# A plain small unit first in every half step of a two-layer encoder, its sums spread behind it, and the first loads paired

## The chip, the cores and the metric

The kernel runs on one core of one Trainium2 chip. The metric is the device time of one execution in microseconds (us). Three runs of the kernel before took 1905.81, 1903.66 and 1898.64 us, median 1903.66 us. A profile was taken of one more execution.

## What the kernel must compute

The input x is 512 tokens of 1024 channels in float32. Each of two layers does three residual steps on it, and a last RMSNorm ends the network:

```
x = x + 0.5 * SwiGLU_1(RMSNorm(x))        # "ffn1": 1024 -> 2816 gate and up -> 1024
h = RMSNorm(x); p = h @ W_in              # pooling group, and q, k, v of 12 heads of 64
x = x + concat(pool(p), attention(p)) @ W_out
x = x + 0.5 * SwiGLU_2(RMSNorm(x))        # "ffn2": the same form, other weights
SwiGLU(h) = (silu(h @ w_gate) * (h @ w_up)) @ w_down
```

## The kernel before, in words

The residual is held transposed, as eight tiles x[0] to x[7] of 128 channels by 512 tokens. Every float32 product is made of three fp32r matmuls: each operand is split into a high part (a rounded copy, ScalarE) and a low part (the rest, VectorE). For a weight piece of 128 x 1024 these are `whi` (L374) and `wlo` (L377), made by `divide`; `take` asks for the next piece and divides two pieces ahead, and `pump` starts loads on the SyncE queue as long as buffers are free.

A SwiGLU works through its 2816 columns in six units, `UNITS` = (5, 0, 1, 2, 3, 4). Units 0 to 4 have 512 gate and 512 up columns each and use a 2 x 2 Strassen-Winograd scheme with seven products (`products`, order `PORD`); unit 5, the small unit, has 256 and 256 columns and comes first. In ffn1 it is done by `plain_unit`: four token blocks t, eight channel chunks k, three matmuls of 512 columns each, 96 in all, with four PSUM banks of tags A, A, B, B; its weights come as four pieces g of two chunks each. In ffn2 it is done by `products` with matmuls of 256 columns, 168 in all.

The Strassen products need x in parts (`Norm.fold`). For each chunk c, ScalarE first writes a scaled copy `xs` = x[c] * gain (L445). Chunks 0 to 3 give the parts `ah`, `al` of the first token half (and, in ffn1 only, `a2` of the second half). Chunks 4 to 7 give `ah`, `al` of both halves, and then at once the four sums and differences of the halves of chunks c - 4 and c: four VectorE instructions of 256 columns (L470 to L473), two ScalarE copies into `sh` (L476, L477), and two VectorE rests into `sl` (L480, L481). `ah` and `al` serve products 1, 2 and 4, and the plain unit; `sh` and `sl` serve products 6, 5, 7 and 3. `fold` runs inside the loop that finishes the step before: in `startup`, in the output projection of the mixing step (`residual`, L997), or in the last down projection (L765).

The order of instructions on each engine is the order in which the program writes them. Work that is to come a little later is put on three lists: `flush` runs the list `later`, and then `lazy` moves up to `later` and `slow` to `lazy`. `finish_col` flushes twice, then has TensorE reduce the squares (L527), VectorE add epsilon (L529) and GpSimd take the power -0.5 (L530); `activation_block` needs that result for silu (L624) and the gating product (L625), which free a PSUM bank. After the small unit its activated columns are transposed (`turn`, L632) during the unit that follows.

`startup` loads x in eight DMAs and the first four weight pieces between them, `vecs` (the gains), `col` and the positions on the GpSimd queue. It runs ten idle matmuls, then folds all eight chunks, while only the first two weight pieces are divided there; the third is divided when `plain_unit` first asks.

Of the kernel before, what the change touches and what calls it, by code (L numbers as in the profile page):

```python
# [36 lines left out]
NU = 5  # L37
# [41 lines left out]
def trunk(ctx: ExitStack, tc: tile.TileContext, a: dict):  # L79
# [20 lines left out]

    x = [const.tile([P, S], F32, name=f"x{c}") for c in range(KD)]
    vecs = const.tile([P, a["vecs"].shape[1]], F32, name="vecs")
# [16 lines left out]
    def startup(norm):  # L119
        nc.sync.dma_start(x[0], a["xT"][0])  # L120
        load(2)
        nc.gpsimd.dma_start(vecs, a["vecs"])
        nc.vector.memset(ones, 1.0 / D)
        nc.vector.memset(npow, -0.5)
        idle = const.tile([P, S], mybir.dt.bfloat16, name="idle")
        nc.vector.memset(idle, 0.0)
        nc.scalar.activation(npow, npow, AF.Copy)
        nc.sync.dma_start(x[1], a["xT"][1])
        nc.sync.dma_start(x[2], a["xT"][2])
        load(2)  # L130
# [7 lines left out]
        pos = a["positions"]  # L138
        nc.gpsimd.dma_start(col, a["col"])
        nc.gpsimd.dma_start(pos_i, bass.AP(tensor=pos.tensor, offset=pos.offset, ap=[[0, P], [1, S]]))  # L140
        warm = bank("D", "warm")
        for _ in range(WARM):
            nc.tensor.matmul(warm, idle[:, 0:P], idle, start=True, stop=True)
        for c in range(KD):
            norm.fold(c)
            if c < 4:
                divide(c % 2)
            flush()
            if c > 0:
                norm.square(c - 1)  # L150
        norm.square(KD - 1)

    def tables():
# [20 lines left out]


        nc.vector.tensor_copy(ang, pos_i)
        nc.vector.tensor_scalar(ang, ang, col[:, 0:1], None, op0=ALU.mult)
# [64 lines left out]
    def product_jobs(i, l, u):  # L242

        small = u == NU
        cps = 1 if small else 2
        made, out = {}, []

        def quarter(kh, n, cp):
            ap = a[f"gs{i}"][l, kh, n] if small else a[f"gu{i}"][l, u, kh, n, cp]
            made[kh, n, cp] = Load(ap, D)  # L250

# [62 lines left out]
    def ffn_jobs(i, l):  # L314
        for n, u in enumerate(UNITS):
            if i == 1 and u == NU:
                for g in range(4):
                    plain(("c", l, g), a["gc"][l, g], D)
# [19 lines left out]

    def load(pieces=1):
        ld = loads[state["load"]]  # L340
        ld.tile = t4([P, ld.n], F32, f"raw{state['load']}")
        state["load"] += 1
        state["live"] += 1
        state["temps"] += ld.temps
        for z in range(pieces):
            o, e = z * ld.n // pieces, (z + 1) * ld.n // pieces
            nc.sync.dma_start(ld.tile[:, o:e], ld.src[:, o:e])

# [77 lines left out]
    class Norm:  # L426
# [11 lines left out]
        def fold(self, c):  # L438

            H = S // 2  # L440
            if c == 0:
                self.xs, self.ah, self.al, self.sh, self.sl, self.a2 = ([None] * 4 for _ in range(6))
            k, nm = c % 4, f"{self.name}_{c}"
            xs = t2([P, 2, H], F32, f"xs_{nm}")
            nc.scalar.activation(xs.rearrange("p b t -> p (b t)"), x[c], AF.Copy, scale=gain(self.n, c))  # L445
            if c < 4:
                self.xs[k] = xs
                hi, lo = t3([P, 3, H], F32R, f"ah_{nm}"), t3([P, 3, H], F32R, f"al_{nm}")
                self.ah[k], self.al[k] = hi, lo
                nc.scalar.activation(hi[:, 0, :], xs[:, 0, :], AF.Copy)  # L450
                later.append(lambda: nc.vector.tensor_tensor(lo[:, 0, :], xs[:, 0, :], hi[:, 0, :].bitcast(F32),
                                                             op=ALU.subtract))
                if self.n % 3 == 0:
                    a2 = t2([P, 2, H], F32R, f"a2_{nm}")
                    self.a2[k] = a2
                    nc.scalar.activation(a2[:, 0, :], xs[:, 1, :], AF.Copy)
                    later.append(lambda: nc.vector.tensor_tensor(a2[:, 1, :], xs[:, 1, :], a2[:, 0, :].bitcast(F32),
                                                                 op=ALU.subtract))
                return
            hi, lo, x1 = self.ah[k], self.al[k], self.xs[k]  # L460
            self.xs[k] = None
            nc.scalar.activation(hi[:, 1:3, :], xs, AF.Copy)
            s13, s24 = t2([P, 2, H], F32, f"s13_{nm}"), t2([P, 2, H], F32, f"s24_{nm}")
# [4 lines left out]
            def sums():  # L468
                tt(lo[:, 1:3, :], xs, hi[:, 1:3, :].bitcast(F32), op=ALU.subtract)
                tt(s13[:, 0, :], x1[:, 1, :], xs[:, 1, :], op=ALU.subtract)  # L470
                tt(s24[:, 0, :], s13[:, 0, :], x1[:, 0, :], op=ALU.subtract)
                tt(s13[:, 1, :], x1[:, 0, :], x1[:, 1, :], op=ALU.subtract)
                tt(s24[:, 1, :], xs[:, 0, :], s24[:, 0, :], op=ALU.add)  # L473

# [141 lines left out]
    def ffn(which, l, norm, nxt, first=False):  # L616
# [20 lines left out]
        def products(n, u):  # L637
            N = S if u < NU else S // 2
            w, cps = N // 2, 2 if u < NU else 1
            xs = [bank("BA"[n % 2], f"px_{nm}_{u}_{i}") for i in range(2)]  # L640
# [7 lines left out]
            def evacuate(p):  # L648
                add, sub = ALU.add, ALU.subtract
                for i in range(2):  # L650
# [4 lines left out]
                    elif p == 2:  # L655
                        nc.vector.tensor_tensor(c[11, i], Z, c[11, i], op=add)
                        if n:
                            lazy.append(lambda i=i: activation_block(c[11, i], c[11, i], i, w))
                    elif p == 6:
                        nc.scalar.activation(new(12, i), X, AF.Copy)  # L660
                        if not n:
                            activation_block(c[11, i], c[11, i], i, w)
                    elif p == 5:
                        nc.scalar.activation(new(22, i), Z, AF.Copy)
                    elif p == 7:
                        nc.vector.tensor_tensor(c[22, i], c[22, i], X, op=sub)
                        later.append(lambda i=i: activation_block(c[22, i], c[22, i], 2 + i, w))
                    elif p == 3:
                        nc.vector.tensor_tensor(c[12, i], Z, c[12, i], op=sub)  # L669
                        later.append(lambda i=i: activation_block(c[12, i], c[12, i], i, w))  # L670
                    else:
                        activation_block(new(21, i), X, 2 + i, w)

            def step(p, cp):
# [5 lines left out]
                out = zs if p in (2, 5, 3) else xs  # L680
                ks = range(2 * cp, 2 * cp + 2) if cps == 2 else range(4)
                for i in range(2):
# [10 lines left out]
                if cp == cps - 1:  # L693
                    if not n and p == 6:
                        norm.finish_col()
                    evacuate(p)
# [4 lines left out]
            for p in PORD:  # L701
                for cp in range(cps):
                    step(p, cp)
                    if turns and z >= 1:
                        for _ in range(2):
                            if turns:
                                turns.pop(0)()
                    if n and z in DOWN_AT[last]:
                        flush()
# [9 lines left out]
            if n:  # L719
                for z, dp in enumerate(todo):  # L720
                    flush()
                    down(UNITS[n - 1], dp)
                    if last:
                        for _ in range(2):
                            flush()
                            turns.pop(0)()

        def plain_unit(u):
# [41 lines left out]
        for n, u in enumerate(UNITS):  # L770
            if n == 0 and which == 1:
                plain_unit(u)
# [384 lines left out]
```

## Time and profile before

| | us |
|---|---|
| median of three runs | 1903.66 |
| the profiled execution, as a run | 1906.05 |
| its span, first to last instruction | 1903.9 |
| TensorE busy | 1854.1 (97%) |
| VectorE busy | 1422.6 (75%) |
| ScalarE busy | 942.6 (50%) |
| mean granted TensorE clock | 0.987 |

The busy time of TensorE counts matmuls whose ends are modelled, so a share near 100% does not mean that it runs at its peak. A granted clock of 1.00 is 2.4 GHz, 0.50 is 1.2 GHz. The idle time named behind a row is that of its engine just before it, with what ended it.

### The profile page before, as it was taken

Reading aid. Unit: us, or ns where it says so; the run is one execution under the profiler, and the core shown is the slowest. Engines: PE = TensorE matmul, PEld = TensorE weight load, DVE = VectorE, ACT = ScalarE, POOL = GpSimd, SP = SyncE. Lnnn points to the kernel's source line nnn. Section 1 sums busy time; section 2 is a strip of 40 time slices with the busy share of each in tenths; the row PEclk is TensorE's granted clock in tenths of the full one; section 3 lists DMA queues with packets and bytes.
Section 4 is the critical chain, followed back from the end, with each engine's and each line's share of the span. In section 5 each row is a group of like instructions: output and inputs, shape, how many; then the busy total and the mean of one; then the engine's idle time right before and its main releaser. Section 6 shows DMA issues by size and latency. Waiting matters only on the chain.

```text
span 1903.9 us, 23219 instructions
## 1 busy us (share of the span) xinstructions
PE 1854.1 (97%) x8822; PEld 1542.4 (81%) x8822; DVE 1422.6 (75%) x2016; ACT 942.6 (50%) x1457; POOL 117.0 (6%) x105
## 2 busy tenths in 40 slices
PE   5999999999998999999999999999999989999998
PEld 4888888898877888888878888888888778888887
DVE  5898677747887886677678777766688688777675
ACT  5444444526665544344555444444467564444344
POOL 0000000014230000000000000000323100000000
PEclk8999999999999999999999999999999989999999
DMA  5322333144441232333313332330544223323321
GB/s 190 106 96 81 111 131 107 43 128 117 111 139 57 90 110 99 122 103 109 110 34 114 130 100 89 100 127 17 152 122 138 78 83 117 107 92 100 100 78 45
DMA packets 59838, 194.33 MB, mean 102 GB/s; under 512 B 7936, under 2 KB 8080, under 8 KB 59728
## 3 DMA queue, kind: packets, MB, share of 16 engines
q1 hardware_dynamic: 59584, 192.57, 31.8%
q8 instruction: 69, 1.13, 0.2%
q0 software_dynamic: 144, 0.29, 0.1%
q14 instruction: 41, 0.34, 0.1%
HBM read 171.87 MB, written 2.10 MB: 91 GB/s over the span
## 4 chain that ended last, share of the span: by engine, by line
PE 89%; DVE 7%; ACT 2%; issue 1%; DMA 0%; SPq 0%; DVEq 0%; POOLq 0%; POOL 0%; ACTq 0%
PE pd_f L401 8%; PE pd_f L400 8%; PE pd_f L399 8%; PE px_f L690 8%; PE px_f L687 8%; PE px_f L689 8%; PE pz_f L687 6%; PE pz_f L690 6%; PE pz_f L689 6%; PE pv_m L807 4%; PE ps_m L874 2%; PE pt_m L887 2%; PE pt_f L632 2%; DVE wlo L377 1%; PE pp_q_m L399 1%
## 5 line engine op out<-in xcount | busy, mean ns | idle before, releaser
L377 DVE TENSOR_TENSOR wlo<-raw,whi 128x1024 fp32r<-128x1024 f32 (+2 forms) x418 | 496.4, 1194 | 50.2 <-ACT whi L374 40.7
L374 ACT ACTIVATE whi<-raw 128x1024 fp32r<-128x1024 f32 (+2 forms) x418 | 417.9, 1024 | 222.3 <-DVE wlo L377 68.9
L401 PE MATMUL pd_f<-ah_f,wlo 128*128 128x512 f32 (+1 forms) x736 | 281.2, 382 | 2.0 <-DVE wlo L377 2.0
L399 PE MATMUL pd_f<-ah_f,whi 128*128 128x512 f32 (+1 forms) x736 | 280.8, 382 | 1.0 <-ACT ah_f L417 1.0
L400 PE MATMUL pd_f<-al_f,whi 128*128 128x512 f32 (+1 forms) x736 | 280.2, 381 | 1.0 <-DVE al_f L420 1.0
L765 DVE SCALAR_TENSOR_TENSOR x<-pd_f,x 128x512 f32<-128x512 f32 x184 | 127.0, 690 | 168.1 <-PE pd_f L401 164.6
L624 ACT ACTIVATE c_f<-c_f,rcol_n 128x256 f32<-128x256 f32 (+1 forms) x132 | 65.7, 500 | 244.4 <-DVE c_f L669 90.8
L401 PEld LDWEIGHTS pd_f<-ah_f,wlo 128*128 128x128 f32 x736 | 138.4, 188 | 32.1 <-DVE wlo L377 6.6
L400 PEld LDWEIGHTS pd_f<-al_f,whi 128*128 128x128 f32 x736 | 138.4, 188 | 28.6 <-DVE al_f L420 2.3
L399 PEld LDWEIGHTS pd_f<-ah_f,whi 128*128 128x128 f32 x736 | 138.4, 188 | 27.3 <-ACT ah_f L417 1.9
L687 PE MATMUL px_f<-whi,sh_n 128*128 128x512 f32 (+1 forms) x352 | 135.6, 385 | 1.4 <-ACT c_f L654 1.4
L690 PE MATMUL px_f<-wlo,sh_n 128*128 128x512 f32 (+1 forms) x352 | 135.3, 384 | 0.1
L689 PE MATMUL px_f<-whi,sl_n 128*128 128x512 f32 (+1 forms) x352 | 135.1, 384 | 0.0
L687 PE MATMUL pz_f<-whi,sh_n 128*128 128x512 f32 (+1 forms) x352 | 133.7, 380 | 0.0
L690 PE MATMUL px_f<-wlo,ah_n 128*128 128x512 f32 (+1 forms) x352 | 133.6, 380 | 0.0
L689 PE MATMUL px_f<-whi,al_n 128*128 128x512 f32 (+1 forms) x352 | 133.6, 379 | 0.0
L687 PE MATMUL px_f<-whi,ah_n 128*128 128x512 f32 (+1 forms) x352 | 133.6, 379 | 0.0
L690 PE MATMUL pz_f<-wlo,sh_n 128*128 128x512 f32 (+1 forms) x352 | 133.5, 379 | 0.0
L689 PE MATMUL pz_f<-whi,sl_n 128*128 128x512 f32 (+1 forms) x352 | 133.5, 379 | 0.0
L879 ACT ACTIVATE e_m<-e_m,nmx_m 128x512 f32<-128x512 f32 x96 | 69.4, 723 | 79.2 <-DVE nmx_m L877 78.6
L877 DVE CUSTOM_DVE_ANT_0 e_m<-ps_m,gbias 128x512 f32<-128x512 f32 x96 | 65.8, 686 | 33.7 <-PE ps_m L874 33.1
L530 POOL TENSOR_TENSOR rcol_n<-rcol_n,npow 128x4 f32<-128x4 f32 x6 | 6.1, 1016 | 1238.2 <-DVE rcol_n L529 1238.2
(224 smaller groups left out, 3665.8 us busy)
## 6 DMA issues: line engine op xcount, KB each, us to landing
raw<-in_gu SPq DMA_DIRECT2D x160, 512.0 KB, 3.3
raw<-in_dn SPq DMA_DIRECT2D x80, 512.0 KB, 3.3
raw<-in_wqk SPq DMA_DIRECT2D x24, 512.0 KB, 5.6
qq_m<-hl_q_m SPq DMA_DIRECT2D x48, 256.0 KB, 4.4
raw<-in_wo SPq DMA_DIRECT2D x16, 512.0 KB, 5.0
raw<-in_wv SPq DMA_DIRECT2D x16, 384.0 KB, 3.1
kk_m<-hl_k_m SPq DMA_DIRECT2D x48, 128.0 KB, 2.3
raw<-in_ds SPq DMA_DIRECT2D x16, 256.0 KB, 2.6
```

Of the source, the lines that this page charges most:

```text
L374: nc.scalar.activation(hi[:, o:e], raw[:, o:e], AF.Copy)
L377: nc.vector.tensor_tensor(lo[:, o:e], raw[:, o:e], hi[:, o:e].bitcast(F32), op=ALU.subtract)
L399: nc.tensor.matmul(ps, hi[:, o:o + P], act[0], start=start, stop=False)
L400: nc.tensor.matmul(ps, hi[:, o:o + P], act[1], start=False, stop=False)
L401: nc.tensor.matmul(ps, lo[:, o:o + P], act[0], start=False, stop=stop)
L687: nc.tensor.matmul(ps, bh, hi[:, o], start=(k == 0 and p in (1, 2, 5)), stop=False, skip_group_check=True)
L689: nc.tensor.matmul(ps, bl, hi[:, o], start=False, stop=False, skip_group_check=True)
L690: nc.tensor.matmul(ps, bh, lo[:, o], start=False, stop=(k == 3), skip_group_check=True)
L765: nc.vector.scalar_tensor_tensor(x[d], ps, 0.5, x[d], op0=ALU.mult, op1=ALU.add)
L807: nc.tensor.matmul(ps[t][:, :384], h[k][p_][:, t * P:(t + 1) * P], q_[:, o:o + 384], start=(k == 0 and n == 0), stop=(k == KD - 1 and n == 2))
L877: nc.vector.tensor_tensor_reduce(e, ps, gbias[:, o:o + S], -0.125, 3.0e38, ALU.add, ALU.min, nmx[hd][:, it:it + 1])
L879: nc.scalar.activation(e, e, AF.Exp, bias=nmx[hd][:, it:it + 1], scale=-1.0, accum_out=den[hd][:, it:it + 1])
```

## The change

In both ffn1 and ffn2 the first unit is now `plain_unit`, so the second form of the small unit is gone from `products` and from the arrays. `fold` no longer writes `xs`: the parts come straight from x with the gain as scale (ScalarE for the high part, one `scalar_tensor_tensor` on VectorE for the low part), and `a2` is made in every half step. The sums move out of `fold` into `sums(k)`, which first writes scaled copies `x1` and `x2` of chunks k and k + 4; it is called behind weight pieces 1 and 2 of the plain unit and behind token blocks 0 and 1 of its last piece. In `startup`, x[0] and x[1] are loaded in front of the two halves of the first weight piece, the other chunks in pairs of 512 KB (rows of 4 KB) with one weight piece behind each pair; the third and fourth pieces are divided in chunks 4 and 6; `col` and the positions are loaded later, in the first step of the rotary tables.

```diff
     def startup(norm):
-        nc.sync.dma_start(x[0], a["xT"][0])
-        load(2)
         nc.gpsimd.dma_start(vecs, a["vecs"])
+        load(2, first=0)
...
-        nc.sync.dma_start(x[1], a["xT"][1])
-        nc.sync.dma_start(x[2], a["xT"][2])
-        load(2)
-        nc.sync.dma_start(x[3], a["xT"][3])
-        for c in range(4, KD):
-            if c % 2 == 0:
-                load()
-            nc.sync.dma_start(x[c], a["xT"][c])
+        for c in range(1, 4):
+            nc.sync.dma_start(xp[c].rearrange("p c t -> p (c t)"), a["xT"][c])
+            load()
...
             if c < 4:
                 divide(c % 2)
+            elif c % 2 == 0:
+                divide()
...
+            def part(hi, lo, src):
+                nc.scalar.activation(hi, src, AF.Copy, scale=g)
+                later.append(lambda: nc.vector.scalar_tensor_tensor(lo, src, g, hi.bitcast(F32),
+                                                                    op0=ALU.mult, op1=ALU.subtract))
+            if c < 4:
...
+                part(self.ah[k][:, 0, :], self.al[k][:, 0, :], x[c][:, 0:H])
+                part(self.a2[k][:, 0, :], self.a2[k][:, 1, :], x[c][:, H:S])
+            else:
+                flat = lambda t: t[:, 1:3, :].rearrange("p b t -> p (b t)")
+                part(flat(self.ah[k]), flat(self.al[k]), x[c])
+
+        def sums(self, k):
+            x1, x2 = t2([P, 2, H], F32, f"x1_{nm}"), t2([P, 2, H], F32, f"x2_{nm}")
+            for t, c in ((x1, k), (x2, k + 4)):
+                nc.scalar.activation(t.rearrange("p b t -> p (b t)"), x[c], AF.Copy, scale=gain(self.n, c))
...
             for g in range(3):
                 flush()
-                w = take("c", l, g)
+                w = take("c", which, l, g)
                 for z in range(2):
                     for t in range(4):
                         part(t, 2 * g + z, w, z * S)
                     flush()
-            w = take("c", l, 3)
+                if g:
+                    norm.sums(g - 1)
+            flush()
+            w = take("c", which, l, 3)
             norm.finish_col()
...
                 activation_block(cs[t], ps[t], t, S // 2)
+                if t < 2:
+                    norm.sums(t + 2)
...
         for n, u in enumerate(UNITS):
-            if n == 0 and which == 1:
+            if n == 0:
                 plain_unit(u)
```

## Rows read from the trace of the kernel before

**Rows 1.** The page's chain that ended last, its shares by engine.
```profile
PE 89%; DVE 7%; ACT 2%; issue 1%; DMA 0%; SPq 0%; DVEq 0%; POOLq 0%; POOL 0%; ACTq 0%
```
**Rows 2.** Windows over first units: length, PE, PEld, DVE, ACT, POOL busy (instructions), clock, DMA, GB/s.
```profile
6.89:51.09 44.20, 27.64 (x105) 20.93 (x106) 28.44 (x53) 25.82 (x44) 1.03 (x1) 0.81 0.46 174
604.54:636.31 31.77, 26.19 (x178) 24.86 (x177) 26.93 (x44) 18.54 (x33) 1.02 (x1) 0.84 0.24 76
957.56:986.38 28.82, 26.13 (x105) 20.81 (x104) 19.36 (x33) 12.43 (x19) 1.01 (x1) 0.88 0.09 28
```
**Rows 3.** Windows around falls of the granted clock, and behind a plain unit.
```profile
612.90:623.10 10.20, 8.62 (x35) 7.74 (x36) 9.83 (x16) 6.20 (x11) 0.00 (x0) 0.50 0.15 51
968.60:971.70 3.10, 0.73 (x2) 0.30 (x2) 3.10 (x5) 3.10 (x4) 0.00 (x0) 0.94 0.32 85
971.70:978.10 6.40, 6.08 (x14) 4.79 (x15) 3.67 (x4) 1.20 (x2) 0.00 (x0) 0.50 0.01 3
986.38:1000.90 14.52, 14.52 (x70) 12.11 (x69) 12.92 (x13) 7.19 (x10) 0.00 (x0) 1.00 0.11 31
```
**Rows 4.** TensorE timeline (start, length, instruction), and the chain's piece for the squares.
```profile
985.70 0.39 PE L735 MATMUL pc_f<-whi,ah_n 128*128 128x512 f32 x1
986.38 0.39 PE L687 MATMUL px_f<-whi,ah_n 128*128 128x512 f32 x1
636.08 0.40 PE L687 MATMUL px_f<-whi,ah_n 128*128 128x512 f32 x1
980.15 0.79 PE ms_n L527 x8
```
**Rows 5.** VectorE timeline at the first layer's ffn2, from the first residual add on.
```profile
585.70 0.69 DVE L997 TENSOR_TENSOR x<-po_m,x 128x512 f32<-128x512 f32 x1 [4.42 <-PE po_m L401]
...
608.56 0.42 DVE L470 TENSOR_TENSOR s_n<-xs_n,xs_n 128x256 f32<-128x256 f32 x1
...
610.03 1.22 DVE L377 TENSOR_TENSOR wlo<-raw,whi 128x1024 fp32r<-128x1024 f32 x1
611.16 0.68 DVE L997 TENSOR_TENSOR x<-po_m,x 128x512 f32<-128x512 f32 x1
...
612.36 0.69 DVE L480 TENSOR_TENSOR sl_n<-s_n,sh_n 128x512 fp32r<-128x512 f32 x1
```
**Rows 6.** ScalarE: timeline of the first chunk, and two pieces of the chain.
```profile
4.85 0.72 ACT L445 ACTIVATE xs_n<-x,vecs 128x512 f32<-128x512 f32 x1 [2.61 <-DMA vecs<-in_vecs]
5.60 0.42 ACT L450 ACTIVATE ah_n<-xs_n 128x256 fp32r<-128x256 f32 x1
...
6.23 0.61 ACT L374 ACTIVATE whi<-raw 128x512 fp32r<-128x512 f32 x1
...
616.44 0.52 ACT sh_n L477
616.96 0.96 ACT whi L374
```
**Rows 7.** What follows the plain unit: power, table load, silu, first weight rest.
```profile
L530 POOL TENSOR_TENSOR rcol_n<-rcol_n,npow 128x4 f32<-128x4 f32 x6 | 6.1, 1016 | 1238.2 <-DVE rcol_n L529 1238.2
47.23 1.28 ACT L624 ACT_TABLE_LOAD   x1 [9.50 <-PE pc_f L737]
982.54 0.48 ACT L624 ACTIVATE cc_f<-pc_f,rcol_n 128x256 f32<-128x256 f32 x1 [9.49 <-PE pc_f L737]
988.04 1.22 DVE L377 TENSOR_TENSOR wlo<-raw,whi 128x1024 fp32r<-128x1024 f32 x1 [0.47 <-ACT whi L374]
```
**Rows 8.** DMA: queues (packets, MB, share) at 6 to 7 us; x[1]'s landing; a window.
```profile
q0 software_dynamic: 33, 0.12, 41.8%
q1 hardware_dynamic: 44, 0.07, 25.3%
...
x<-in_xT SPq DMA_DIRECT2D x1, 256.0 KB, 7.7
...
10.00:20.00 10.00, 8.27 (x35) 6.42 (x35) 6.41 (x14) 9.84 (x20) 0.00 (x0) 1.00 1.04 405
```

More of the change, by code (lines that the diff above doesn't have):

```diff
@@ L98, in bank @@
         return psum.tile([P, S], F32, tag=tag, name=name, bufs=2)
-    x = [const.tile([P, S], F32, name=f"x{c}") for c in range(KD)]
+    xp = [const.tile([P, 2, S], F32, name=f"x{c}") for c in range(KD // 2)]
+    x = [xp[c // 2][:, c % 2, :] for c in range(KD)]
     vecs = const.tile([P, a["vecs"].shape[1]], F32, name="vecs")
@@ L147, in startup @@
                 divide(c % 2)
+            elif c % 2 == 0:
+                divide()
             flush()
-            if c > 0:
-                norm.square(c - 1)
-        norm.square(KD - 1)
+            norm.square(c)
     def tables():
@@ L173, in reduce @@
             yield
+        pos = a["positions"]
+        nc.gpsimd.dma_start(col, a["col"])
+        nc.gpsimd.dma_start(pos_i, bass.AP(tensor=pos.tensor, offset=pos.offset, ap=[[0, P], [1, S]]))
+        yield
         nc.vector.tensor_copy(ang, pos_i)
@@ L242, in product_jobs @@
     def product_jobs(i, l, u):
-        small = u == NU
-        cps = 1 if small else 2
+        cps = 2
         made, out = {}, []
         def quarter(kh, n, cp):
-            ap = a[f"gs{i}"][l, kh, n] if small else a[f"gu{i}"][l, u, kh, n, cp]
-            made[kh, n, cp] = Load(ap, D)
+            made[kh, n, cp] = Load(a[f"gu{i}"][l, u, kh, n, cp], D)
         quarters = [(0, 0), (1, 0)]
@@ L315, in ffn_jobs @@
         for n, u in enumerate(UNITS):
-            if i == 1 and u == NU:
+            if n == 0:
                 for g in range(4):
-                    plain(("c", l, g), a["gc"][l, g], D)
+                    plain(("c", i, l, g), a[f"gc{i}"][l, g], D)
                 continue
@@ L337, in trunk, with load @@
         ffn_jobs(2, l)
-    def load(pieces=1):
+    def load(pieces=1, first=None):
         ld = loads[state["load"]]
@@ L346, in load @@
             o, e = z * ld.n // pieces, (z + 1) * ld.n // pieces
+            if first is not None:
+                nc.sync.dma_start(x[first + z], a["xT"][first, :, z * S:(z + 1) * S])
             nc.sync.dma_start(ld.tile[:, o:e], ld.src[:, o:e])
@@ L441, in fold @@
             if c == 0:
[L442 to L445, printed above, removed]
-            if c < 4:
[L447 to L459, printed above, removed]
@@ L460, in fold @@
-            hi, lo, x1 = self.ah[k], self.al[k], self.xs[k]
-            self.xs[k] = None
-            nc.scalar.activation(hi[:, 1:3, :], xs, AF.Copy)
+                self.ah, self.al, self.sh, self.sl, self.a2 = ([None] * 4 for _ in range(5))
+            k, g, nm = c % 4, gain(self.n, c), f"{self.name}_{c}"
+            def part(hi, lo, src):
+                nc.scalar.activation(hi, src, AF.Copy, scale=g)
+                later.append(lambda: nc.vector.scalar_tensor_tensor(lo, src, g, hi.bitcast(F32),
+                                                                    op0=ALU.mult, op1=ALU.subtract))
@@ L468, in sums @@
             def sums():
-                tt(lo[:, 1:3, :], xs, hi[:, 1:3, :].bitcast(F32), op=ALU.subtract)
-                tt(s13[:, 0, :], x1[:, 1, :], xs[:, 1, :], op=ALU.subtract)
+                tt(s13[:, 0, :], x1[:, 1, :], x2[:, 1, :], op=ALU.subtract)
                 tt(s24[:, 0, :], s13[:, 0, :], x1[:, 0, :], op=ALU.subtract)
                 tt(s13[:, 1, :], x1[:, 0, :], x1[:, 1, :], op=ALU.subtract)
-                tt(s24[:, 1, :], xs[:, 0, :], s24[:, 0, :], op=ALU.add)
+                tt(s24[:, 1, :], x2[:, 0, :], s24[:, 0, :], op=ALU.add)
             def parts():
@@ L656, in evacuate @@
                         nc.vector.tensor_tensor(c[11, i], Z, c[11, i], op=add)
-                        if n:
-                            lazy.append(lambda i=i: activation_block(c[11, i], c[11, i], i, w))
+                        lazy.append(lambda i=i: activation_block(c[11, i], c[11, i], i, w))
                     elif p == 6:
                         nc.scalar.activation(new(12, i), X, AF.Copy)
-                        if not n:
-                            activation_block(c[11, i], c[11, i], i, w)
                     elif p == 5:
@@ L680, in step @@
                 out = zs if p in (2, 5, 3) else xs
-                ks = range(2 * cp, 2 * cp + 2) if cps == 2 else range(4)
+                ks = range(2 * cp, 2 * cp + 2)
                 for i in range(2):
@@ L693, in step @@
                 if cp == cps - 1:
-                    if not n and p == 6:
-                        norm.finish_col()
                     evacuate(p)
@@ L707, in products @@
                                 turns.pop(0)()
-                    if n and z in DOWN_AT[last]:
+                    if z in DOWN_AT[last]:
                         flush()
@@ L718, in products @@
                         u, f, [c[top, 0], c[top, 1], c[low, 0], c[low, 1]], j, w))
[L719 to L726, printed above, removed]
+            for dp in todo:
+                flush()
+                down(UNITS[n - 1], dp)
+                if last:
+                    for _ in range(2):
+                        flush()
+                        turns.pop(0)()
         def plain_unit(u):
@@ L770, in ffn @@
         for n, u in enumerate(UNITS):
-            if n == 0 and which == 1:
+            if n == 0:
                 plain_unit(u)
@@ L1117 @@
         arrays[f"gu{i}"] = big.transpose(0, 6, 1, 7, 2, 4, 3, 5, 8).reshape(L, NU, 2, 2, 2, P, D)
-        small = pair[..., NB:]
-        if i == 1:
-            arrays["gc"] = small.reshape(L, 4, 2, P, S).transpose(0, 1, 3, 2, 4).reshape(L, 4, P, D)
-        else:
-            arrays["gs2"] = small.reshape(L, 2, 4, P, 2, 2, P).transpose(0, 1, 5, 3, 2, 4, 6).reshape(L, 2, 2, P, D)
+        small = pair[..., NB:].reshape(L, 4, 2, P, S)
+        arrays[f"gc{i}"] = small.transpose(0, 1, 3, 2, 4).reshape(L, 4, P, D)
         dn = v[f"ffn{i}_w_down"]
```

12 lines of the change are left out of this document (6 added, 6 removed).

## The prediction, written before the changed kernel was timed

> **What bounds the kernel now.** I read the page first. Its chain that ended last is 89% TensorE and 7% VectorE [rows 1], so time can only be won where TensorE waits, or runs at half clock, for something the change touches. The list of the chain in order of time shows such places at four stretches only, the first units of the four half steps; I then asked for a window over each [rows 2]. At startup the plain unit stands from 6.89 to 51.09, 44.2 us. In the first layer's ffn2 the Strassen small unit starts at 604.54 and the next unit at 636.08 [rows 4], 31.5 us. In the second layer's ffn1 the plain unit takes 28.8 us. The second layer's ffn2 repeats the first's within 0.3 us. The reader is to hold these against TensorE's own need. Three matmuls of 512 columns step by 0.68 us [rows 4], so one is 0.227 and a plain unit is 96 x 0.227 = 21.8 us; with the eight little matmuls of the squares, 0.79, it is 22.6. The excess is 21.6, 6.2 and, for ffn2 made plain, 8.9 us. In each stretch VectorE is nearly always busy and TensorE waits for it; after the wait the clock falls to 0.50 (1.2 GHz) [rows 3].
>
> **Prices.** Steps are taken from start to start. VectorE: the four sums of one k 1.47, a weight rest of 1024 columns 1.13, any 512-wide instruction 0.60 [rows 5]; 256 wide, about 0.35. ScalarE: 256 wide 0.32, 512 wide 0.52, a weight piece 0.96 [rows 6]. The new low parts are `scalar_tensor_tensor` instead of `tensor_tensor`, and are made from x with a scale. No row of this form from this source is in this stretch; the bounds are the 0.60 of a 512-wide tensor_tensor and the 0.69 length of the residual add, at most 0.09 apart and 0.7 us over eight of them, and I take 0.60.
>
> **What goes, what comes.** Per half step `fold` loses eight `xs` copies (8 x 0.52), but `sums` writes eight of them again: ScalarE does the same work later. VectorE's sums (4 x 1.47) and their rests (8 x 0.60), 10.7 us, also move, from in front of the plain unit to inside it. ffn2 gains four `a2` pairs (each 0.32 on ScalarE and 0.35 on VectorE) and loses, with the Strassen form, three weight splits and four weight sums, 7 x 1.13 = 7.9 us of VectorE, and 2.9 of ScalarE.
>
> **ffn2, first layer.** VectorE's queue from 585.70 to 604.54 [rows 2, 5] after the change: eight residual adds, four low parts of 512 and seven square sums at 0.60 (11.4), eight low parts of 256 (2.8), four weight rests (4.5): 18.7 us for 18.8 us. So the last residual add, which ran at 611.16 with VectorE 6.6 us behind, runs when TensorE has finished its input, about 604.8. It matters now: the plain unit's second bank is the one this add reads (tag A; before, the unit took B). TensorE has three matmuls (0.7 us) in front of that bank, so it waits 0.3 us. Then 72 x 0.227 + 0.79 + 24 x 0.227: the unit ends at 627.4, 8.7 us earlier than 636.08. No wait for weights inside: the third piece's rest is done near 609 and wanted at 615.
>
> Behind it a new wait appears. From the last residual add at 605.4 VectorE has a low part, a square sum, four weight rests and, for sums 0 and 1, 2 x (1.47 + 1.2): 11.1 us, some 12 with two handovers from ScalarE; so these are done by 618, before the squares at 622. Token block 0 ends at 623.3; the table load of 1.28 follows and silu 0.48 [rows 7]: 625.1. Then, in program order: copies for sum 2 to 626.3, its sums on VectorE to 627.7, the parts on ScalarE to 628.9, parts of sum 3 to 630.9, silu of block 3 to 631.3; on VectorE rests 2 to 630.9, gating product, rests 3 to 632.5, last gating product to 633.0. Only then come the weights of the next unit: a rest (1.13), a weight sum of two instructions (2.3), a rest, two activation rests (1.2), a second weight sum, and the rest that product 6 wants: 9.2 us, 642.2. TensorE has 48 matmuls and 8 transposes in front of it (10.9 + 0.9) and could begin it at 639.7. So it waits 2.5 us. In the second layer's ffn1 VectorE started the same list 1.66 us behind the unit [rows 4, 7], and here 5.6 behind: that is where the wait is from. Net gain 8.7 - 2.5 = 6.2, and 5.9 in the second layer's ffn2: 12.1 us.
>
> **ffn1, second layer.** Without the sums VectorE has per chunk of the last down projection at most 1.9 us + 0.57 of weight rests, TensorE 12 x 0.227 = 2.7: no backlog. The unit ends at 957.56 + 22.6 = 980.2 instead of 986.38, 6.2 earlier. The same chain behind it, but without a table load, costs 2.5 - 1.3 = 1.2. Net 5.0 us.
>
> **Startup.** `vecs` lands at 4.85 and starts everything, as before; without `xs` the first matmul moves from 6.89 to about 6.1. ScalarE then sets the pace: 0.32 + 0.32 + 0.52 + 0.52 for each of chunks 0 to 3, 1.04 for each of 4 to 7, and two pieces of 0.96: 12.8 us. x[1], now third in the queue, has no row there. In its old place it took 7.7 us [rows 8]; x[0] was in before 4.85. I take 4 us after an issue at 1.7, between them, because from 6 to 7 us the positions on the other queue took 41.8% of the engines and left 25.3% [rows 8], and they now come later. The first pair has no row either: 1.5 MB must have passed. At 405 GB/s [rows 8] all the way that is 6 us, with 7.7 from its issue near 2.6 it is 10.3; I take 9.7, near the upper end, as loads are issued close together, and 11.3 for its weights. Then what is left of chunks 2 to 7 (8.8 us) ends on ScalarE at 20.3 with the handovers, TensorE goes on at 12.3 without a break (72 x 0.227 + 0.79), and the unit ends at 29.5: 21.6 us earlier, since the third weight piece is no longer split behind all sums.
>
> The Trainium skill ("DMA: Bandwidth & Descriptors", Specifications) gives 512 bytes as the least transfer at full rate; x's rows were 2 KB already. By it the pairs save nothing, the first pair lands no earlier than 10.3, and startup gains 0.6 us less.
>
> Here the chain behind is longer, because ScalarE arrives late: copies 0 to 21.4, a weight piece, parts 0 to 24.1, copies 1 to 25.2, a weight piece, parts 1 to 27.9, rests 1 to 29.2. The reciprocal root waits behind these rests on VectorE and takes 1.0 on GpSimd [rows 7]: silu begins at 30.4 and frees the first bank at 31.5, the second at 34.0. TensorE wants them at 29.5 and 32.9: waits of 2.0 and 1.1, then 0.6 for the last gating product, and 2.5 for the weights as above: 6.2. I add 1 us because the clock may fall there. Net 21.6 - 7.2 = 14.4 us. The position load lies at the start of the next unit, GpSimd being free by then, and costs nothing; if it were late, VectorE would stand before the tables for up to the 7.7 us of a load.
>
> **The sum.** 12.1 + 5.0 + 14.4 = 31.5 us off the profiled execution of 1906.05 us (span 1903.9 and 2.2 around it): 1874.5. The median of the runs stands 2.4 below that execution, so I predict 1872.
>
> **Rivals.** (1) The sums hide wholly: the chains behind the unit run beside product 1 without loss, gain 21.6 + 8.7 + 8.4 + 6.2 = 44.9, time 1859. For it: TensorE's first two products need no sum. Against: behind the second layer's plain unit VectorE was busy 12.9 us of 14.5 without them [rows 3], so room is small. 20%.
> (2) The clock falls behind each plain unit. For it: in the second layer's ffn1 waits that left TensorE 0.73 us of work in 3.1 sufficed [rows 3]; startup's two waits are alike. Price: a fall lasts 6.4 to 10.2 us, half of that is lost, 3 to 5, less what the wait for weights hides: 3 each, 12 in all: 1884. The Trainium skill ("TensorE: Matmul & The Clock Gate", Part 1) has the clock gated down by idleness and released by activity, which is this rival; the trace agrees on the two levels. 17%.
> (3) The loads set startup: pairs land 3 to 4 us later than taken, and the weight pieces behind them again, startup gains 7 instead of 14.4: 1880. For it x[1]'s 7.7. Against: 405 GB/s from 10 us on. 15%.
> (4) Slower: the four sums run in series behind the unit (1.1 + 1.5 + 1.1 + 1.2 = 4.9 each, 19.6), the weights' 9.2 behind them, 28.8 against the 12.3 that TensorE has: 16.5 lost, and 5 by the clock, in four places 86, less 44.9: 1945. It decides from a loss of 11.2 us a place. Against: two of four sums are written ahead of the last weight piece, where ScalarE and VectorE stand idle before. 4%.
>
> **How the numbers follow.** The forecast has 44%. The range 1857 to 1889 takes in rivals 1 to 3 with the error of a few us at startup, and leaves out rival 4 and the tails. What a measurement can tell from no change is 0.5%, 9.5 us: only rival 4, or most chains failing at once, is not faster. Faster 0.94, same 0.02, slower 0.04.
>
> **What would show it.** After: TensorE's first unit-0 matmul near 29.5 and idle beside it for banks; ffn2's plain unit about 23 us long at clock 1.00; waits of 2 to 3 us for `wlo` at product 6; VectorE busy through the plain unit's second half. Wrong: a clock of 0.50 inside a plain unit, a wait of TensorE on x's landing past 12 us, or a first unit in ffn2 over 28 us.

## The result, and the profile after

The changed kernel takes 1876.93 us (median of 4 runs, 1876.34 to 1877.6), the kernel before 1904.74 us (4 runs, 1898.64 to 1906.01): a ratio of 0.987, interval 0.9857 to 0.9882. The forecast was 1872, faster, in a range of 1857 to 1889. So 27.8 us came off by the medians where 31.5 were forecast, and 28.1 us between the two profiled spans (1903.9 and 1875.8). By the ratio of the runs it is 24.8 us (22.5 to 27.2). The profiled execution of the kernel before (1906.05 as a run) is slower than all its timed runs, so what is read from the two traces below lies at the upper end.

The chain that ended last has the shares of before [rows 1] within a point, TensorE 89% and VectorE 7% of the span; they don't show where 28 us went. A place in the program that both kernels pass does. In the first Strassen unit I take the first matmul of product 6 that uses the rests of the weights, and call it the mark: up to it the edits of a half step have had nearly all their effect. TensorE's timeline of the kernel before (start, length, instruction, what it waited for), at the four marks:

```profile
63.35 0.39 PE L690 MATMUL px_f<-wlo,sh_n 128*128 128x512 f32 x1
...
648.35 0.39 PE L690 MATMUL px_f<-wlo,sh_n 128*128 128x512 f32 x1
...
998.61 0.39 PE L690 MATMUL px_f<-wlo,sh_n 128*128 128x512 f32 x1
...
1580.51 0.39 PE L690 MATMUL px_f<-wlo,sh_n 128*128 128x512 f32 x1
```

The same timeline of the kernel after, with the first matmul, the last one of the first plain unit (31.25), the waits with a bracket between each plain unit and its mark, and the start of the last plain unit (1514.18):

```profile
7.09 0.80 PE L725 MATMUL pc_f<-whi,ah_n 128*128 128x512 f32 x1 [1.39 <-ACT whi L370]
...
31.25 0.39 PE L727 MATMUL pc_f<-wlo,ah_n 128*128 128x512 f32 x1
33.14 0.51 PE L680 MATMUL px_f<-whi,ah_n 128*128 128x512 f32 x1 [1.50 <-DVE cc_f L622]
...
35.82 0.50 PE L680 MATMUL px_f<-whi,ah_n 128*128 128x512 f32 x1 [1.01 <-DVE cc_f L622]
...
45.14 0.50 PE L683 MATMUL pz_f<-wlo,ah_n 128*128 128x512 f32 x1 [0.47 <-DVE wlo L373]
...
49.87 0.50 PE L683 MATMUL px_f<-wlo,sh_n 128*128 128x512 f32 x1 [1.71 <-DVE wlo L373]
...
624.37 0.50 PE L683 MATMUL pz_f<-wlo,ah_n 128*128 128x512 f32 x1 [0.51 <-DVE wlo L373]
...
629.09 0.50 PE L683 MATMUL px_f<-wlo,sh_n 128*128 128x512 f32 x1 [1.70 <-DVE wlo L373]
...
975.16 0.51 PE L683 MATMUL px_f<-wlo,sh_n 128*128 128x512 f32 x1 [1.54 <-DVE wlo L373]
...
1514.18 0.39 PE L725 MATMUL pc_f<-whi,ah_n 128*128 128x512 f32 x1
...
1547.82 0.50 PE L683 MATMUL pz_f<-wlo,ah_n 128*128 128x512 f32 x1 [0.52 <-DVE wlo L373]
...
1552.54 0.50 PE L683 MATMUL px_f<-wlo,sh_n 128*128 128x512 f32 x1 [1.71 <-DVE wlo L373]
```

The lead at the four marks is 13.5, 19.3, 23.4 and 28.0 us, and 28.1 at the end: the time was won in the four stretches of the forecast and nowhere else. The first units began at 604.54 and 957.56 before [rows 2] (and at 1536.97), which gives the lead with which each half step starts, and so what each one adds from its start to its mark:

| | from start to mark, before | after | gain | forecast |
|---|---|---|---|---|
| startup, to the next half step's start | | | 13.8 | 14.4 |
| ffn2, first layer | 43.8 | 38.4 | 5.45 | 6.2 |
| ffn1, second layer | 41.05 | 36.65 | 4.4 | 5.0 |
| ffn2, second layer | 43.5 | 38.4 | 5.2 | 5.9 |

The gains add up to 28.85; 0.2 and 0.7 us were lost between one mark and the next start, and nothing in the rows says why. One execution is not exact to a microsecond: the kernel with the form alone (below) has the startup of before and passes the first mark at 61.90, 1.45 us earlier than the 63.35 of before.

The windows over the plain units and over the stretches from them to the marks (length; PE, PEld, DVE, ACT, POOL busy; granted clock; DMA; GB/s):

```profile
31.64:49.87 18.23, 13.54 (x59) 9.89 (x59) 16.40 (x26) 12.29 (x21) 1.54 (x3) 1.00 0.10 29
590.73:613.88 23.15, 23.02 (x105) 18.84 (x104) 14.31 (x26) 13.64 (x20) 1.02 (x1) 1.00 0.00 1
613.88:629.09 15.21, 13.00 (x59) 9.86 (x57) 15.11 (x24) 9.72 (x17) 0.00 (x0) 1.00 0.07 18
938.51:961.22 22.71, 22.71 (x106) 18.92 (x104) 15.84 (x29) 13.62 (x21) 1.01 (x1) 1.00 0.00 0
961.22:975.16 13.94, 12.40 (x60) 10.03 (x58) 13.84 (x20) 8.61 (x15) 0.00 (x0) 1.00 0.07 21
```

Against 31.5 us (604.54 to 636.08 [rows 4]) and 28.8 us [rows 2] before, the units of ffn2 and ffn1 are 23.15 and 22.71 us long, full of matmuls, at clock 1.00 (2.4 GHz). The stretches behind them are where VectorE is now the late one: 15.11 of 15.21 and 13.84 of 13.94 us busy, and TensorE waits for it. VectorE's timeline behind the first layer's ffn2 shows why, line by line:

```profile
590.97 0.68 DVE L992 TENSOR_TENSOR x<-po_m,x 128x512 f32<-128x512 f32 x1
...
608.47 0.16 DVE L526 TENSOR_SCALAR rcol_n<-ms_n 128x4 f32<-128x4 f32 x1 [4.33 <-PE ms_n L524]
611.83 0.48 DVE L622 SCALAR_TENSOR_TENSOR cc_f<-pc_f,rcol_n,cc_f 128x256 f32<-128x256 f32 x1 [3.19 <-ACT cc_f L621]
...
619.57 1.21 DVE L373 TENSOR_TENSOR wlo<-raw,whi 128x1024 fp32r<-128x1024 f32 x1
...
627.82 1.22 DVE L373 TENSOR_TENSOR wlo<-sum,whi 128x1024 fp32r<-128x1024 f32 x1
```

With sums 0 and 1 done VectorE stands idle for 4.33 and 3.19 us, and only then gets sums 2 and 3, ahead of the weights that TensorE waits for. The list of the weights begins at 619.57, 5.7 us behind the end of the unit.

### The profile page after: what moved, and what is told of

Its sections match the earlier page's. It is cut to its first block, busy times and chain, and to the rows that moved or that the text cites. A ratio compares the mean times of both kernels' runs of the same rounds, so it can differ in the third digit from the quotient of the medians.

```text
span 1875.8 us, 22885 instructions
## 1 busy us (share of the span) xinstructions
PE 1846.1 (98%) x8678; PEld 1527.9 (81%) x8678; DVE 1404.7 (75%) x1990; ACT 933.5 (50%) x1439; POOL 117.0 (6%) x105
## 4 chain that ended last, share of the span: by engine, by line
PE 89%; DVE 7%; issue 2%; ACT 1%; DMA 1%; SPq 0%; POOL 0%; DVEq 0%; POOLq 0%; ACTq 0%
PE pd_f L397 8%; PE pd_f L396 8%; PE pd_f L395 8%; PE px_f L683 7%; PE px_f L680 7%; PE px_f L682 7%; PE pz_f L683 5%; PE pz_f L680 5%; PE pz_f L682 5%; PE pv_m L802 4%; PE ps_m L869 2%; PE pt_m L882 2%; DVE wlo L373 2%; PE pt_f L629 2%; PE pp_q_m L395 1%
## 5 line engine op out<-in xcount | busy, mean ns | idle before, releaser
L621 ACT ACTIVATE c_f<-c_f,rcol_n 128x256 f32<-128x256 f32 x120 | 61.2, 510 | 234.5 <-DVE c_f L662 87.5
L397 PEld LDWEIGHTS pd_f<-ah_f,wlo 128*128 128x128 f32 x736 | 138.4, 188 | 31.5 <-DVE wlo L373 6.0
L683 PE MATMUL px_f<-wlo,sh_n 128*128 128x512 f32 x320 | 125.1, 391 | 6.7 <-DVE wlo L373 6.7
L680 PE MATMUL px_f<-whi,ah_n 128*128 128x512 f32 x320 | 124.8, 390 | 2.5 <-DVE cc_f L622 2.5
L683 PE MATMUL px_f<-wlo,ah_n 128*128 128x512 f32 x320 | 124.7, 390 | 0.0
L680 PE MATMUL px_f<-whi,sh_n 128*128 128x512 f32 x320 | 124.7, 390 | 0.0
L682 PE MATMUL px_f<-whi,sl_n 128*128 128x512 f32 x320 | 124.6, 389 | 0.0
L682 PE MATMUL px_f<-whi,al_n 128*128 128x512 f32 x320 | 124.6, 389 | 0.0
L682 PE MATMUL pz_f<-whi,sl_n 128*128 128x512 f32 x320 | 124.6, 389 | 0.0
L680 PE MATMUL pz_f<-whi,sh_n 128*128 128x512 f32 x320 | 124.6, 389 | 0.0
L683 PE MATMUL pz_f<-wlo,sh_n 128*128 128x512 f32 x320 | 124.6, 389 | 0.0
```

Source lines behind the costliest of these rows:

```text
L397: nc.tensor.matmul(ps, lo[:, o:o + P], act[0], start=False, stop=stop)
L680: nc.tensor.matmul(ps, bh, hi[:, o], start=(k == 0 and p in (1, 2, 5)), stop=False, skip_group_check=True)
L682: nc.tensor.matmul(ps, bl, hi[:, o], start=False, stop=False, skip_group_check=True)
L683: nc.tensor.matmul(ps, bh, lo[:, o], start=False, stop=(k == 3), skip_group_check=True)
```

## Experiments

Theory A is the forecast: each half step's gain is the sums gone from in front of the first unit, less a wait that the last two sums cause behind it. Its rivals here: that the plain form itself, the loads' order or the third weight piece's early split carries the gain, or that the clock takes part of it. The form alone, the loads, the early split alone and the early sums were timed on one chip, the other four on a second, the kernel after on another occasion, so small differences are given by the ratios to the kernel before as well.

**The form alone.** The kernel before, with ffn2 plain too and all else as it was (a `fold` with the `a2` pairs everywhere, sums still in front):

```diff
...
-            if i == 1 and u == NU:
+            if n == 0:
...
-                    plain(("c", l, g), a["gc"][l, g], D)
+                    plain(("c", i, l, g), a[f"gc{i}"][l, g], D)
...
-                if self.n % 3 == 0:
+                if True:
...
-            if n == 0 and which == 1:
+            if n == 0:
...
```

> The kernel before with one part of the change alone: ffn2's small unit is plain, but fold still writes xs and makes the sums in front of the unit, and startup is as before. Theory (the time was VectorE's sums standing in front of the first unit): VectorE is as far behind at the end of the mixing step as before (its last residual add near 610 instead of 611), the plain unit's second bank waits for that add, TensorE idles some 5 us and the clock falls; the next unit starts near 636 as before, so 1901 to 1907 us. Rival (the form of the small unit is what gains, with 7.9 us less on VectorE per ffn2): 10 to 12 us faster than before, 1892 to 1895.

Measured 1903.01 us, ratio 1.0006 (0.9996 to 1.0015): nothing gained. TensorE's timeline of this kernel:

```profile
603.64 0.47 PE L735 MATMUL pc_f<-whi,ah_n 128*128 128x512 f32 x1 [0.41 <-DVE x L997]
...
609.23 0.79 PE L735 MATMUL pc_f<-whi,ah_n 128*128 128x512 f32 x1 [4.65 <-DVE x L997]
...
633.38 0.39 PE L687 MATMUL px_f<-whi,ah_n 128*128 128x512 f32 x1
```

Its windows, in the columns of above:

```profile
604.00:610.00 6.00, 1.35 (x5) 0.82 (x4) 5.90 (x12) 4.26 (x8) 0.00 (x0) 0.72 0.21 73
609.23:612.00 2.77, 2.77 (x7) 2.19 (x8) 2.74 (x6) 1.85 (x3) 0.00 (x0) 0.50 0.57 189
```

The unit takes 29.7 us instead of 31.5: TensorE stands 4.65 us for the last residual add, VectorE being 5.90 of 6.00 us busy with the work ahead of it, sums above all, and then runs at a granted clock of 0.50 (1.2 GHz) at first. So the plain form alone brings 1.8 us of the 5.45 in a half step, 3.0 between the profiled spans (1900.9 and 1903.9) and in the medians nothing; what cost is the backlog of sums. The other half alone, the sums moved and the Strassen form kept in ffn2, was not run; there the unit itself multiplies the sums.

**The order of the loads.** The kernel after with the loads of before (single chunks of x, old order, positions and `col` at startup):

```diff
...
-        for c in range(1, 4):
-            nc.sync.dma_start(xp[c].rearrange("p c t -> p (c t)"), a["xT"][c])
-            load()
+        nc.sync.dma_start(x[1], half(1))
+        nc.sync.dma_start(x[2], half(2))
+        load(2)
+        nc.sync.dma_start(x[3], half(3))
+        for c in range(4, KD):
+            if c % 2 == 0:
+                load()
+            nc.sync.dma_start(x[c], half(c))
...
```

> The changed kernel with the loads of before: x in eight pieces in the old order, col and positions loaded at startup. Theory (ScalarE's work and the order of divisions set startup, the loads only its first chunks): x[1] lands near 9.8 again, TensorE idles 1.5 to 2 us behind chunk 0, ScalarE is through chunk 7 about 0.8 us later than 20.2, and the kernel is 0.5 to 1.5 us slower than the changed one: 1877 to 1879. Rival (the paired loads are what startup gains from): 5 us or more slower, over 1881.

Measured 1878.97 us (1878.24 to 1879.82), ratio 0.9877 (0.9862 to 0.9892): 2.0 more than after by the medians, at the upper end of what was expected, and 1.3 by the ratios, whose intervals overlap. The place was expected wrongly: TensorE shows no wait behind chunk 0. Its timeline:

```profile
49.53 0.50 PE L689 MATMUL px_f<-wlo,sh_n 128*128 128x512 f32 x1 [1.71 <-DVE wlo L379]
...
56.38 0.50 PE L403 MATMUL pd_f<-ah_f,wlo 128*128 128x512 f32 x1 [0.67 <-DVE wlo L379]
...
591.45 0.39 PE L731 MATMUL pc_f<-whi,ah_n 128*128 128x512 f32 x1
```

At the mark it is 0.3 us ahead of the kernel after; at 56.38 it is 0.45 us behind (there the kernel after is at 55.93), and 0.7 at the start of the next half step (591.45 against 590.73). That is all of the 0.7 us between the profiled spans (1876.5 and 1875.8); the rest of the 2.0 us no row of the one profiled execution shows. The Trainium skill's figure for the least transfer at full rate ("DMA: Bandwidth & Descriptors", Specifications) gave the pairs no worth; this run changes pairs, order and positions together, so it neither confirms nor denies that.

**The third weight piece's early split.** The kernel after, without it:

```diff
             if c < 4:
                 divide(c % 2)
-            elif c % 2 == 0:
-                divide()
```

> The changed kernel without the division of weight pieces 3 and 4 in chunks 4 and 6 (they are divided when the plain unit asks, but ahead of the sums). Theory (startup gained because the sums no longer stand in front of the third piece's rest): TensorE waits some 3 us near 18 to 21 for the third piece, of which 1 to 3 us remain, since the unit behind waits for VectorE anyway: 1877 to 1880. Rival (the early division is the gain): 8 us or more slower, over 1885.

Measured 1877.62 us, ratio 0.987 (0.9856 to 0.9885): no difference from 1876.93. TensorE waits once inside the unit, 0.89 us where some 3 were expected, and is level with the kernel after again at the mark (49.73 and 49.87):

```profile
21.78 0.50 PE L725 MATMUL pc_f<-wlo,ah_n 128*128 128x512 f32 x1 [0.89 <-DVE wlo L371]
...
49.73 0.51 PE L681 MATMUL px_f<-wlo,sh_n 128*128 128x512 f32 x1 [1.67 <-DVE wlo L371]
```

The 0.89 us is taken out of the waits behind the unit: TensorE does not set the mark.

**Both of these.** The two edits together, so that at startup only the sums' place and the parts made straight from x are new.

> The changed kernel with both parts of startup as before: loads in the old order, and no division of pieces 3 and 4 in chunks 4 and 6. Only the new fold and the spread sums are left of what changes startup. Theory (the sums out of the way are nearly all of startup's 13.5 us): 1878 to 1882. Rival (loads and early division stand in for each other, and one of them is needed): 1888 or more.

Measured 1879.34 us (1878.74 to 1880.87), ratio 0.989 (0.9876 to 0.9903), 2.4 more than after by the medians, 3.8 by the ratios and 1.5 between the spans (1877.3 and 1875.8). TensorE's timeline:

```profile
19.86 0.51 PE L729 MATMUL pc_f<-whi,ah_n 128*128 128x512 f32 x1 [1.77 <-ACT whi L374]
21.84 0.50 PE L731 MATMUL pc_f<-wlo,ah_n 128*128 128x512 f32 x1 [1.25 <-DVE wlo L377]
...
50.19 0.50 PE L687 MATMUL px_f<-wlo,sh_n 128*128 128x512 f32 x1 [1.71 <-DVE wlo L377]
```

Two waits, together 3.0 us, in the unit put the mark back by 0.3 only; at the start of the next half step it is 1.2 (591.95 against 590.73). Of the 13.5 us at startup, loads and early split are worth 1.5 to 3.8; the sums out of the way, and the parts made straight from x that went with them, are the rest.

**The sums earlier.** In all half steps but the first: sum 0 behind piece 1, sum 1 behind piece 2, sums 2 and 3 behind piece 3, none behind the last piece. This takes away the wait that theory A puts behind the unit.

```diff
-                if g:
-                    norm.sums(g - 1)
+                if first:
+                    if g:
+                        norm.sums(g - 1)
+                else:
+                    norm.sums(g)
+                    if g == 2:
+                        norm.sums(3)
...
-                if t < 2:
+                if first and t < 2:
                     norm.sums(t + 2)
```

> The changed kernel with the sums one piece earlier in all half steps but the first: sums 0, 1 and 2, 3 behind pieces 1, 2 and 3 of the plain unit, none in its last piece. Theory (the waits for the low weights of products 2 and 6 behind the plain unit, 0.51 + 1.70, 1.54 and 0.52 + 1.71 us, come from sums 2 and 3 being queued behind the last token blocks): these three places lose their waits, 5 to 6 us, 1871 to 1872, with startup as it is. Rival (VectorE has too little time in the plain unit and the unit behind it together): the waits come back inside the plain unit or stay, 1875 to 1878.

Measured 1869.8 us (1869.05 to 1870.08), ratio 0.9828 (0.9814 to 0.9843): 7.1 less than after by the medians, 8 by the ratios, 7.9 between the spans (1867.9 and 1875.8). TensorE's timeline, the last plain unit's start and its mark:

```profile
1509.29 0.39 PE L725 MATMUL pc_f<-whi,ah_n 128*128 128x512 f32 x1
...
1544.67 0.39 PE L683 MATMUL px_f<-wlo,sh_n 128*128 128x512 f32 x1
```

The window over ffn2's plain unit in the first layer, and those from the end of the first two plain units to the mark (the second starts at 935.49):

```profile
590.80:613.95 23.15, 23.01 (x105) 18.84 (x104) 19.75 (x37) 16.99 (x26) 1.02 (x1) 1.00 0.01 4
613.95:626.19 12.24, 12.24 (x59) 10.21 (x58) 10.65 (x11) 6.80 (x10) 0.00 (x0) 1.00 0.09 23
958.20:970.43 12.23, 12.23 (x60) 10.22 (x58) 10.64 (x11) 6.81 (x10) 0.00 (x0) 1.00 0.10 24
```

No wait is left, the gain is more than the 5 to 6 us expected, and from start to mark the three take 35.4, 34.9 and 35.4 us, 3.0, 1.7 and 3.0 less than in the kernel after. On VectorE the list of the weights begins at 615.61, 1.66 us behind the unit instead of 5.7:

```profile
615.61 1.23 DVE L373 TENSOR_TENSOR wlo<-raw,whi 128x1024 fp32r<-128x1024 f32 x1 [0.46 <-ACT whi L370]
```

This settles the cause of the waits, and prices them: the brackets held 2.2 us in ffn2, the time 3.0.

**The clock at the very start.** The first matmuls of the kernel after step by 0.43 us. Thirteen idle matmuls ahead of them instead of ten (`WARM = 13`).

> The changed kernel with 13 idle matmuls instead of 10, so that TensorE has no idle stretch in front of its first real matmul. In the changed kernel's profile the first real matmuls step by 0.43 us until about 10 us, though the clock column says 1.00. Theory (behind the plain unit TensorE waits for the first bank and then for low weights anyway): the unit ends up to 2 us earlier, the waits behind it grow by as much, 1876 to 1877.5 us, no change. Rival (the slow first matmuls are on the path): 1.5 to 2 us faster, 1875.

Measured 1877.3 us, ratio 0.9878 (0.9865 to 0.9892): no difference. TensorE's timeline:

```profile
32.75 0.50 PE L680 MATMUL px_f<-whi,ah_n 128*128 128x512 f32 x1 [2.07 <-DVE cc_f L622]
```

The unit ends 1.0 us earlier, 0.6 of it goes into a longer wait for the bank (2.07 for 1.50), and the mark is 0.4 earlier. Nor need that be TensorE's doing. The timelines of five kernels, all with the same order of sums at startup, show what the mark follows: VectorE's first sum.

| kernel | gains used by ScalarE | TensorE's first matmul | VectorE's first sum | mark | sum to mark |
|---|---|---|---|---|---|
| after | 5.61 | 7.09 | 22.92 | 49.87 | 26.95 |
| the order of the loads | 5.50 | 6.97 | 22.57 | 49.53 | 26.96 |
| without the early split | 6.30 | 7.78 | 22.77 | 49.73 | 26.96 |
| the sums earlier (not at startup) | 6.53 | 8.01 | 23.06 | 50.01 | 26.95 |
| thirteen idle matmuls | 5.91 | 7.39 | 22.52 | 49.48 | 26.96 |

TensorE begins up to 1.04 us apart, and the mark stands 26.95 or 26.96 us behind that sum each time (27.35 in the kernel with both, where TensorE lost 3.0 us in the unit). At startup VectorE and ScalarE set the mark, not TensorE.

**The best version.** The early sums, and at startup sum 1 only behind the square sums' end, so that the reciprocal root doesn't queue behind its rests on VectorE (the edit against the early sums):

```diff
                 if first:
-                    if g:
-                        norm.sums(g - 1)
+                    if g == 1:
+                        norm.sums(0)
...
             norm.finish_col()
+            if first:
+                norm.sums(1)
```

> The kernel with the sums early in the other half steps (1869.8), and in the first half step sums(1) behind the reduction of the squares instead of ahead of it, so that the reciprocal root does not wait behind sums 1 and their rests on VectorE. Theory (first-bank wait at startup comes from that queue): silu begins near 28.5 instead of 32, the first waits of 1.5 and 1.0 go, three sums instead of two now stand behind the unit, so the waits for low weights stay: 1 to 2 us faster, 1868 to 1869. Rival (ScalarE's total is the limit at startup): no change, 1869 to 1871.

Measured 1868.17 us (1867.63 to 1869.35), ratio 0.983 (0.9817 to 0.9844), 1.6 less than with the early sums alone by the medians; the ratios can't tell them apart. In TensorE's timeline the unit behind begins at 29.63 without a wait, but the wait moves on:

```profile
29.63 0.43 PE L680 MATMUL px_f<-whi,ah_n 128*128 128x512 f32 x1
...
33.46 0.50 PE L680 MATMUL px_f<-whi,ah_n 128*128 128x512 f32 x1 [2.24 <-DVE cc_f L622]
...
47.50 0.50 PE L683 MATMUL px_f<-wlo,sh_n 128*128 128x512 f32 x1 [1.27 <-DVE wlo L373]
```

And the same with thirteen idle matmuls:

> The same with 13 idle matmuls. Theory: with the first bank free in time, the earlier end of the plain unit is worth something only as far as VectorE keeps up: 0 to 1 us on top. Rival: 2 us on top.

Measured 1867.45 us (1867.25 to 1868.51), ratio 0.9828 (0.9815 to 0.9842), the lowest time of all, 9.5 us below the changed kernel by the medians and 8 by the ratios; from the version with ten its range is not separate.

## Why the prediction was right

**Where the time was.** Right, and shown: the form alone gains nothing, the startup of before with only the sums moved and the parts made from x keeps all but 1.5 to 3.8 us, and in the two profiled executions every stretch's gain is within 0.75 us of its forecast. One reading of rows was too strong: over the whole units VectorE was not "nearly always busy" (28.44 of 44.20, 26.93 of 31.77 and 19.36 of 28.82 us [rows 2]); it was so around the waits (3.10 of 3.10, 9.83 of 10.20 [rows 3]).

**ffn2.** The last residual add was to run as soon as TensorE finished its input: VectorE has it at 590.97, as the unit begins at 590.73, and TensorE's fourth matmul follows the third by 0.52 us instead of 0.23 (591.19 and 591.71): the wait of 0.3 us for that add. The unit was forecast 22.9 us long and is 23.15; the weight list 5.6 us behind it, and it is 5.7; the rest for product 6 done 14.8 us behind it, and it is 15.1 (627.82 and 1.13, against 613.88). **ffn1.** The unit was to be 22.6 us and is 22.71.

**The mis-sized term** is the same in these three: the wait behind the unit. It was set at 2.5, 1.2 and 2.5 us and cost 3.0, 1.7 and 3.0, by the experiment that removes it. In ffn2 TensorE starts the mark's matmul 15.2 us behind the unit, 0.14 behind the rest that was forecast for 14.8 and came at 15.1; without a wait it takes 12.24. In ffn1 VectorE's list begins 4.4 us behind the unit (965.63, against 961.22), 1.3 less than in ffn2 as forecast, so it lacks the same 0.5. With the units' 0.1 to 0.3 this is the shortfall of 0.6 to 0.75 in each half step. The brackets show less than was lost, 2.2 in ffn2 (0.51 and 1.70): between 31.25 and 33.14 TensorE loses 1.89 - 0.227 = 1.66 us where the bracket says 1.50, and the step behind is 0.34 instead of 0.227, so 0.27 on top.

**Startup.** Here the forecast of 14.4 for 13.8 is near partly by luck, for it had the wrong engine at the decisive place. ScalarE was to set the pace, and sums 0 to follow its copies, done at 21.4. Two lines of VectorE's timeline of the kernel after, and then ScalarE's:

```profile
21.52 1.48 DVE L509 TENSOR_TENSOR sq_n<-sq_n,sq_n 128x512 f32<-128x512 f32 x2
22.92 0.42 DVE L467 TENSOR_TENSOR s_n<-x_n,x_n 128x256 f32<-128x256 f32 x1
```

```profile
5.61 0.51 ACT L442 ACTIVATE ah_n<-x,vecs 128x256 fp32r<-128x256 f32 x1 [3.37 <-DMA vecs<-in_vecs]
6.03 0.49 ACT L442 ACTIVATE a_n<-x,vecs 128x256 fp32r<-128x256 f32 x1
...
10.85 0.63 ACT L370 ACTIVATE whi<-raw 128x512 fp32r<-128x512 f32 x1 [0.37 <-DMA raw<-in_gc]
...
20.19 1.33 ACT L460 ACTIVATE x_n<-x,vecs 128x512 f32<-128x512 f32 x2
...
24.50 0.63 ACT L473 ACTIVATE sh_n<-s_n 128x512 fp32r<-128x512 f32 x1 [2.03 <-DVE s_n L470]
...
32.09 0.47 ACT L621 ACTIVATE cc_f<-pc_f,rcol_n 128x256 f32<-128x256 f32 x1 [1.09 <-POOL rcol_n L527]
```

The copies do end at 21.4, but VectorE, whose queue up to there the forecast did not write down, comes to the sums at 22.92, behind low parts and square sums, and ScalarE stands 2.03 us for it. From there the chain runs 1.5 to 1.9 us behind its forecast: silu at 32.09 for 30.4, the mark at 49.87 for 47.9 (29.5 + 6.2 + 12.24). Against these 1.9 us stand the 1 us set aside for the clock, which wasn't lost (1.00 in the windows), and 0.3 that came back behind the mark, where the kernel after waits 0.28 us at 55.93 and the kernel before 0.62 at 69.58: 14.4 - 1.9 + 1.0 + 0.3 = 13.8. The unit ends at 31.5 instead of 29.5 (the gains arrived at 5.6 instead of 4.85, and the first eight matmuls stepped at half speed); by the table of five kernels that cost nothing at the mark.

The parts made from x were mis-priced as well. On ScalarE a 256-wide part with the gain steps by 0.40 to 0.42 where 0.32 was taken from a part without one [rows 6]; on VectorE the low parts step by 0.40 and 0.66 where 0.35 and 0.60 were taken. ScalarE reaches the copies at 20.2, as forecast (20.3), because two errors cancel: the parts cost more, and the first pair's weights are in at 10.85 instead of 11.3. How much of VectorE's 1.5 us these prices explain isn't shown. Loads never held TensorE past 7.09.

**The rivals.** (1) The sums don't hide wholly: VectorE is full behind the units, by the waits above. It failed by the order of the sums, not by their amount: put earlier, behind earlier weight pieces, they do hide in three of four places. (2) The clock didn't fall: 1.00 in every window of the kernel after, with waits of 1.5 to 1.7 us in them. The Trainium skill's gate by idleness ("TensorE: Matmul & The Clock Gate", Part 1) isn't refuted: where TensorE stood 4.65 us, in the plain form alone, the granted clock behind it was 0.50. (3) The loads don't set startup: the old ones cost 0.7 to 2.0 us. (4) The chain behind the unit cost 3.0, 1.7 and 3.0 us, and 6.15 at startup (49.87 less 31.48 and 12.24), not 16.5 a place.

**The signs.** ffn2's unit of 23 us at clock 1.00 came, and so did the waits for the weights. One sign did not: VectorE was not busy through the plain unit's second half but idle for 4.33 and 3.19 us in ffn2. The forecast's own reckoning had said as much (sums 0 and 1 done by 618, the squares at 622), and it is the gap that the early sums use. Of the signs of being wrong none came.

What stays open: 0.9 us lost between the half steps, why VectorE was late at startup, and what the old loads cost beyond the 0.7 us in the trace.

## What to carry to other kernels

When work is moved off the path, write the queue of each engine that does it, in program order, up to what the critical engine wants next. The wait that comes back is read from it, here within half a microsecond where VectorE's queue was written, and off by 1.9 at startup where it was not; so is the place (an idle time of that engine a little earlier) where the same work would cost nothing. A wait cost its bracket and 0.2 to 0.4 us more here. A split or load that looks critical inside a unit is worth little when the unit's successor waits for another engine anyway.

## What the runs showed of the hardware

The first matmuls of this kernel ran at half speed in the profiled execution while the granted clock reads 1.00. TensorE's timeline of the kernel after:

```profile
10.56 0.40 PE L727 MATMUL pc_f<-wlo,a_n 128*128 128x512 f32 x1
10.80 0.39 PE L725 MATMUL pc_f<-whi,a_n 128*128 128x512 f32 x1
```

The window over the eight matmuls ahead of these, 3.47 us long:

```profile
7.09:10.56 3.47, 3.47 (x8) 2.72 (x9) 2.69 (x6) 3.24 (x7) 0.00 (x0) 1.00 1.03 417
```

The eight step by 0.43 us on the mean, and from 10.56 on by 0.23 to 0.24, eight matmuls after an idle time of 1.39 us; the clock column doesn't show it, the steps do. With three more idle matmuls ahead they were at 0.23 from 8.45 on. But the best version, with ten idle matmuls and an idle time of 1.49 us before its first real one at 6.51, was at 0.23 from 7.58 on too; what decides it isn't shown.

The landing of the gains (30 KB on GpSimd's queue), which ScalarE's first parts wait for, took from 3.6 to 5.2 us over the ten kernels of this case, though nothing was changed on that load. By the table of five kernels the mark did not follow it: in the kernel after and in the one with the early sums, whose startup is the same, the gains are in use at 5.61 and at 6.53, and it stands at 49.87 and 50.01.
